# A softmax's inverse sums, spread over the partitions by a round trip through DRAM instead of by transposes

## The chip, the core and the metric

The kernel runs on one core of a Trainium2 chip. The core has TensorE (PE, with its weight loads PEld), VectorE (DVE), ScalarE (ACT), GpSimd (POOL) and SyncE (SP); SP and POOL issue the DMAs of this kernel. The metric is the device time of one execution in microseconds. A measurement runs the kernel several times; a profiled execution gives the trace.

## The reference

One encoder block on 2048 tokens of width 1024 with 16 meta tokens ahead of them (2064 in all), in fp32. The part that matters here is the attention: 4 query heads, 2 key and value heads of 128 channels.

```python
def attend(qb):
    s = jnp.einsum('bkgqd,bksd->bkgqs', qb, kt).astype(jnp.float32) * scale
    p = jax.nn.softmax(s, axis=-1).astype(vt.dtype)
    return jnp.einsum('bkgqs,bksd->bkgqd', p, vt)
...
mixed = jnp.concatenate([rms_norm(attn, g_attn_out[i]), rms_norm(four, g_fourier_out[i])], axis=-1)
h = h + mixed @ w_out[i]
m = rms_norm(h, g_mlp[i])
h = h + jnp.square(jax.nn.relu(m @ w_up[i])) @ w_down[i]
```

A Fourier mixing of the other half of the projection stands beside the attention. A normalization at the end gives the output.

## The kernel before, in words

The kernel first projects, normalizes and rotates q, k and v and parks them in DRAM. Then comes the stage of the attention, from about 345 to 990 us, and after it the MLP, whose products take the rest of the time. In the attention stage the units of the attention are interleaved with other work: the Fourier products (`py`, `pa`), then the output projection of the Fourier half (`out_f`, matmuls `pof`, residual tiles `xo`), then that of the attention half (`out_a`, matmuls `poa`, residual tiles `h`). `mix` steps the attention's generator so many steps for each step of the other work.

There are 16 units. A unit is one key and value head with 512 columns: 256 query tokens of 2 heads. The scores `s` of a unit are made transposed, keys on the partitions and queries on the free axis, in 17 steps of 128 keys (the last one is the meta tokens). ScalarE copies each step to `S`; VectorE keeps the running maximum `M` (L783 to L788). When all are there, `stats` turns the maximum over keys into a tile `mb` that has it in every partition. Then `softmax` walks the 17 steps again: VectorE subtracts `mb` (L840), ScalarE takes the exponential (L841), VectorE adds two steps at a time into `acc` (L845, L847), and TensorE multiplies by the values into the PSUM tile `o` (L849). Scores run a unit and a few steps ahead of this.

At a unit's end, `acc` is folded to `sum` (L827, L828), which still has a partial sum in each of the 128 partitions for each of the 512 columns. `finish(u)` is a generator that runs beside the next unit's steps:

1. ScalarE copies the PSUM tile to `O` (L855).
2. `over_keys` (L794, L796) transposes `sum` in four matmuls against the identity into the PSUM tile `pm_l`, and VectorE reduces it to 128 x 4. VectorE's reciprocal makes `rl` of it (L859): the inverse sum of column 128 a + p stands in partition p, place a.
3. `rows_to_cols` (L803) spreads `rl` again: four more transposes of broadcast columns into the PSUM tile `pd_l`, 128 x 512, which has all 512 inverse sums in every partition.
4. VectorE multiplies `O` by it (L861).
5. The result is split into a high and a low part `ohl` (L870 stores them to the DRAM tile `o_d`), and its squares are summed (L872 to L879).

A `yield` stands between these parts; each lets one more step of the next unit be written into the program. `pm_m`, `pd_m`, `pm_l`, `pd_l` and the sums of squares of `out_f` share one PSUM tile, `misc`. The order on each engine is made by a scheduler from the order in which the code is written; each engine runs its own list in order, and SP its list of DMAs in order too. On SP stand, in this stage, the stores of `o_d`, the loads `at` of the attention's output, the loads `xo` and `h` and the stores `h_d` of the residual, the stores `m_d`, and weight loads. POOL issues the loads of q, k and v.

Of the kernel before, what the change touches and what calls it, by code (L numbers as in the profile page):

```python
# [11 lines left out]
F32 = mybir.dt.float32  # L12
R32 = mybir.dt.float32r
AF = mybir.ActivationFunctionType
ALU = mybir.AluOpType
# [4 lines left out]
P = 128  # L20
# [36 lines left out]
def f32v(ap):  # L57
    return ap.bitcast(F32)
# [30 lines left out]
def bc(ap, shape):  # L89
    return ap.broadcast_to(shape)  # L90
# [45 lines left out]
def encoder_block(ctx: ExitStack, tc: tile.TileContext, x, meta, w_in, w_f,  # L136
                  w_out, w_up, w_down, g_fin, g_cols, g_rows, c_id, c_rope, c_dft, c_even, c_odd, c_rem, out):
    nc = tc.nc
# [7 lines left out]
    dram = ctx.enter_context(tc.tile_pool(name="dram", bufs=1, space=DRAM))  # L146
# [445 lines left out]
    for j in range(LAST + 1):  # L592
# [16 lines left out]
        else:  # L609
# [14 lines left out]
            a = 0  # L624
# [67 lines left out]
    ap2 = Lines(tc.alloc_tile_pool(name="ap2", bufs=1, side="right", reuse_waits="tile"), small)  # L692

    def misc(name, shape=(P, 512)):
        return app.tile(list(shape), F32, name=name, tag="misc")
# [18 lines left out]
        return vt  # L714

    o_d = [dram.tile([P, 2, NQ, 512], F32, name=f"o_d{b}") for b in range(4)]
    sqs = {}
    AT = {}

    def a_operand(b, heads):  # L720

        if b not in AT:
            A = AT[b] = ey.tile([P, 2, NQ, 512], R32, name=f"at_{b}", tag=f"e{b % 2}")
            for k in heads:
                for e in range(2):
                    nc.sync.dma_start(f32v(A[:, e, k]), o_d[b][:, e, k])
        return AT[b]

    def attention():
# [60 lines left out]
        def over_keys(x, name, op):  # L790

            ps = misc("pm_" + name, (P, 4, P))
            for a in range(4):
                nc.tensor.transpose(ps[:, a], x[:, a * P:(a + 1) * P], ident)  # L794
            r = ap2.tile([P, 4], F32, name="mx_" + name, tag="mx", bufs=2)
            nc.vector.tensor_reduce(r, ps, axis=AX.X, op=op)  # L796
            return r

        def rows_to_cols(vec, name):

            ps = misc("pd_" + name, (P, 4, P))
            for a in range(4):
                nc.tensor.transpose(ps[:, a], bc(vec[:, a:a + 1], [P, P]), ident)  # L803
            return ps.rearrange("p a e -> p (a e)")
# [46 lines left out]
        def finish(u):  # L851
            b, g = units[u]
            s = state.pop(u)
            O = ap2.tile([P, 512], F32, name=f"O_{u}", tag="Osb", bufs=1)
            nc.scalar.copy(O, s["O"])  # L855
            yield
            sl = over_keys(s["sum"], f"l{u}", ALU.add)
            rl = ap2.tile([P, 4], F32, name=f"rl_{u}", tag="rl", bufs=2)
            nc.vector.reciprocal(rl, sl)  # L859
            yield  # L860
            nc.vector.tensor_tensor(O, O, rows_to_cols(rl, f"l{u}"), op=ALU.mult)  # L861
            c = slice(b % 2 * 256, b % 2 * 256 + 256)
            if u >= len(units) - 2:
                A = a_operand(3, (2, 3))
                split(A[:, 0, 2 * g:2 * g + 2, c], A[:, 1, 2 * g:2 * g + 2, c], O.rearrange("p (h n) -> p h n", h=2))
            else:
                hl = ap2.tile([P, 2, 512], R32, name=f"ohl_{u}", tag="ohl", bufs=1)
                split(hl[:, 0], hl[:, 1], O)
                for e in range(2):
                    nc.sync.dma_start(o_d[b // 2][:, e, 2 * g:2 * g + 2, c],  # L870
                                      f32v(hl[:, e]).rearrange("p (h n) -> p h n", h=2))
            nc.scalar.square(O, O)  # L872
            first = b not in sqs
            if first:
                sqs[b] = ap2.tile([P, 256], F32, name=f"sq_{b}", tag="sq", bufs=6)
                nc.vector.tensor_tensor(sqs[b], O[:, :256], O[:, 256:], op=ALU.add)
            else:
                for h in range(2):
                    nc.vector.tensor_tensor(sqs[b], sqs[b], O[:, h * 256:(h + 1) * 256], op=ALU.add)  # L879
# [27 lines left out]
        for n in range(total):  # L907
            u, i = divmod(n, K)
            for g in list(later):
                if next(g, "end") == "end":  # L910
                    later.remove(g)
            softmax(u, i)
            loads_next("v", u, i)
            if i == NT:
                later.append(finish(u))
                next(later[-1])
            more(n + 1 + K + LEADT)
            yield
# [816 lines left out]
```

## Time and profile before

| what | us |
|---|---|
| median of 3 runs | 2256.97 |
| the three runs | 2256.97, 3771.39, 2255.45 |
| the profiled execution's own time | 2255.64 |
| its span, first to last instruction | 2253.6 |
| start of the first and of the last transpose of L803 for `pd_l` | 385.0, 988.2 |

The run of 3771.39 stands alone and no profile was taken of it. The profile's lines come from one execution; the span leaves out 2.0 us around the first and the last instruction. In the lines that follow, a group of instructions has its engine, the line of the program, the operation, what it writes and reads, and the durations; a line of the timeline begins with its start and duration in us. A matmul's duration reaches past the start of the next one, since matmuls are pipelined. A line of the windows gives the stretch, its length, and the busy time of each engine with the number of instructions.

### The profile page before, as it was taken

What the parts mean: (1) busy time and instruction counts of PE and PEld (TensorE: products, weight loads), DVE (VectorE), ACT (ScalarE), POOL (GpSimd) and SP (SyncE); (2) the same over time, 40 slices, a digit from 0 to 9 for tenths busy, and PEclk for the clock granted to TensorE, in tenths of its full rate; (3) what the DMA queues carried; (4) which work ended last, traced back from release to release, by engine and by line L of the source; (5) the groups of instructions that cost most, each with busy time, mean ns of one, the idle gap of its engine ahead of it and who ended that gap; (6) DMA issues with size and microseconds to landing.
All of it is one profiled execution on the core that took longest, in us unless ns stands there. A gap on an engine that the chain in (4) does not pass through costs nothing.

```text
span 2253.6 us, 28116 instructions
## 1 busy us (share of the span) xinstructions
PE 2233.3 (99%) x10238; PEld 1771.3 (79%) x10238; DVE 1692.9 (75%) x2250; ACT 1178.1 (52%) x1997; POOL 247.8 (11%) x285
## 2 busy tenths in 40 slices
PE   9999999999999999999999999999999999999998
PEld 7898987766667666677888888888888888888887
DVE  6334579999999889788677668788765656796795
ACT  6443356666555566668556563334455545443343
POOL 2212120003322122110000020000110000200000
PEclk9999999999999999999999999999999999999999
DMA  6332253123344434357777576445594444954342
GB/s 205 90 108 70 86 149 90 52 65 130 113 133 131 158 128 133 137 208 256 264 233 241 181 290 227 132 143 167 185 362 169 154 154 152 343 178 159 126 137 84
DMA packets 191786, 367.40 MB, mean 163 GB/s; under 512 B 15760, under 2 KB 74768, under 8 KB 189984
## 3 DMA queue, kind: packets, MB, share of 16 engines
q1 hardware_dynamic: 171040, 310.08, 40.8%
q0 software_dynamic: 20464, 55.27, 7.6%
q8 instruction: 80, 1.31, 0.2%
q14 instruction: 58, 0.48, 0.1%
q10 hardware_dynamic: 144, 0.26, 0.0%
HBM read 236.28 MB, written 129.27 MB: 162 GB/s over the span
## 4 chain that ended last, share of the span: by engine, by line
PE 89%; DVE 5%; ACT 2%; DMA 1%; issue 1%; POOL 1%; SPq 0%; POOLq 0%; ACTq 0%; DVEq 0%
PE o L849 7%; PE ux L82 5%; PE ux L80 5%; PE ux L81 5%; PE dx L82 5%; PE dx L81 5%; PE dx L80 5%; PE dy L82 4%; PE dy L81 4%; PE dy L80 4%; PE uy L82 4%; PE uy L80 4%; PE uy L81 4%; PE s L80 2%; PE s L82 2%; PE s L81 2%
## 5 line engine op out<-in xcount | busy, mean ns | idle before, releaser
L70 ACT CAST ah<-a 128x1024 fp32r<-128x1024 f32 x108 | 113.0, 1050 | 263.2 <-PE dx L81 108.5
L849 PE MATMUL o<-S,vn 128*128 128x512 f32 x512 | 243.6, 596 | 4.2 <-ACT S L841 3.4
L780 ACT COPY S<-s 128x512 f32<-128x512 f32 x256 | 145.0, 584 | 92.4 <-PE s L82 73.1
L82 PE MATMUL dx<-bh,al 128*128 128x512 f32 x496 | 192.5, 388 | 0.0
L81 PE MATMUL dx<-bl,ah 128*128 128x512 f32 x496 | 192.5, 388 | 0.0
L80 PE MATMUL dx<-bh,ah 128*128 128x512 f32 x496 | 192.5, 388 | 0.0
L82 PE MATMUL ux<-bf,wul 128*128 128x512 f32 x448 | 174.2, 389 | 0.7 <-DVE wul L71 0.7
L80 PE MATMUL ux<-bf,wuh 128*128 128x512 f32 x448 | 174.6, 390 | 0.0
L81 PE MATMUL ux<-bf,wuh 128*128 128x512 f32 x448 | 174.3, 389 | 0.0
L840 DVE TENSOR_TENSOR S<-S,mb 128x1024 f32<-128x1024 f32 x128 | 155.1, 1227 | 11.7 <-ACT mb L811 11.6
L841 ACT ACTIVATE S<-S 128x1024 f32<-128x1024 f32 x128 | 135.1, 1062 | 43.0 <-DVE S L840 41.8
L71 DVE TENSOR_TENSOR al<-a,ah 128x1024 fp32r<-128x1024 f32 x108 | 131.2, 1219 | 31.6 <-ACT ah L70 31.3
L849 PEld LDWEIGHTS o<-S,vn 128*128 128x128 f32 x512 | 92.1, 189 | 75.2 <-issue 59.0
L80 PE MATMUL dy<-bh,ah 128*128 128x512 f32 (+1 forms) x388 | 150.5, 388 | 0.0
L81 PE MATMUL dy<-bl,ah 128*128 128x512 f32 (+1 forms) x388 | 150.5, 388 | 0.0
L82 PE MATMUL dy<-bh,al 128*128 128x512 f32 (+1 forms) x388 | 150.5, 388 | 0.0
L80 PE MATMUL s<-q,kt 128*128 128x512 f32 (+1 forms) x272 | 145.3, 534 | 2.3 <-ACT S L780 2.0
L80 PE MATMUL uy<-bf,wuh 128*128 128x512 f32 x320 | 125.0, 391 | 0.3 <-ACT wuh L70 0.3
L82 PE MATMUL uy<-bf,wul 128*128 128x512 f32 x320 | 124.6, 390 | 0.7 <-DVE wul L71 0.7
L81 PE MATMUL uy<-bf,wuh 128*128 128x512 f32 x320 | 124.8, 390 | 0.0
L786 DVE TENSOR_TENSOR M<-M,S 128x1024 f32<-128x1024 f32 x96 | 117.6, 1225 | 8.9 <-ACT S L780 8.0
L1212 ACT ACTIVATE c<-c 128x512 f32<-128x512 f32 x96 | 60.5, 631 | 119.4 <-DVE c L1260 116.6
(323 smaller groups left out, 5708.3 us busy)
## 6 DMA issues: line engine op xcount, KB each, us to landing
a<-s_d SPq DMA_DIRECT2D x84, 512.0 KB, 3.7
R<-in_w_up_dram SPq DMA_DIRECT2D x32, 1024.0 KB, 5.5
s_d<-s SPq DMA_DIRECT2D x128, 256.0 KB, 2.1
s_d<-c SPq DMA_DIRECT2D x96, 256.0 KB, 2.7
d<-in_w_down_dram SPq DMA_DIRECT2D x48, 512.0 KB, 5.2
f_d<-lf SPq DMA_DIRECT2D x56, 256.0 KB, 2.8
bf<-f_d SPq DMA_DIRECT2D x7, 2048.0 KB, 14.3
a<-s_d POOLq DMA_DIRECT2D x24, 512.0 KB, 7.3
```

What stands on the lines that cost most here:

```text
L70: self.high = nc.scalar.copy(hi, src)
L71: self.low = nc.vector.tensor_tensor(lo, src, f32v(hi), op=ALU.subtract)
L80: nc.tensor.matmul(out, a[0], b[0], start=first, stop=False, skip_group_check=chain)
L81: nc.tensor.matmul(out, a[0], b[1], start=False, stop=False, skip_group_check=chain)
L82: nc.tensor.matmul(out, a[1], b[0], start=False, stop=last, skip_group_check=chain)
L780: nc.scalar.copy(S[:, i % 2], ps)
L786: nc.vector.tensor_tensor(M, M, S, op=ALU.max)
L840: nc.vector.tensor_tensor(S, S, mb, op=ALU.subtract)
L841: nc.scalar.activation(p, S, AF.Exp, scale=ISQ)
L849: nc.tensor.matmul(s["O"], v[:, 2 * j % 4 + e], p[:, e], start=i + e == 1, stop=False)
L1212: nc.scalar.activation(dst, src, AF.Relu)
```

## The change

In the first 15 units, part 3 is replaced. `rl` is written to a row of 512 floats in DRAM, one such row for each unit, element by element: partition p, place a goes to place 128 a + p. A second DMA reads that row back into all 128 partitions of a new SBUF tile `rb`. Both are issued by SP, and the second waits until the first has landed. The generator then yields three times instead of once before the product, so that two more steps of the next unit are written ahead of it. The last unit does as before.

```diff
+    l_d = [dram.tile([1, 512], F32, name=f"l_d{u}") for u in range(15)]
...
             nc.vector.reciprocal(rl, sl)
-            yield
-            nc.vector.tensor_tensor(O, O, rows_to_cols(rl, f"l{u}"), op=ALU.mult)
+            if u < len(l_d):
+                nc.sync.dma_start(l_d[u].rearrange("o (a p) -> p (o a)", p=P), rl)
+                over = ap2.tile([P, 512], F32, name=f"rb_{u}", tag="rb", bufs=1)
+                nc.sync.dma_start(over, l_d[u].broadcast_to([P, 512]))
+                for _ in range(3):
+                    yield
+            else:
+                yield
+                over = rows_to_cols(rl, f"l{u}")
+            nc.vector.tensor_tensor(O, O, over, op=ALU.mult)
```

The scheduler then orders the engines anew in this stage. On TensorE, around the group of unit 1, before (`pd_l1` is the group, `py2` a Fourier product, `o_2` the product with the values of unit 2):

```order
L82 MATMUL s_3_5_4374<-q_3_4133,kt_2_1_3789 128x512
L849 MATMUL o_2_4340<-S_2_0_3929,vn_2_0_4036 128x512
L803 MATMUL pd_l1_4350<-ident_96,rl_1_4337 128x128 x4
L849 MATMUL o_2_4340<-S_2_0_3929,vn_2_0_4036 128x512
L82 MATMUL py2_2_0_4380<-thi2_3_4069,alo2_3_4112 128x258
```

and now:

```order
L795 MATMUL pm_l1_4343<-ident_96,sum_1_4329 128x128 x4
L81 MATMUL py2_2_0_4382<-tlo2_3_4084,ahi2_3_4123 128x258
L82 MATMUL py2_2_0_4382<-thi2_3_4082,alo2_3_4125 128x258
L850 MATMUL o_2_4356<-S_2_0_3944,vn_2_0_4049 128x512 x2
L587 MATMUL py2_2_0_4382<-thi2_4_4088,ahi2_4_4132 128x258
```

The group is gone, and the two matmuls of `o_2` that it parted stand together. On VectorE, from the reciprocal of unit 2 on, before:

```order
L859 RECIPROCAL rl_2_4674<-mx_l2_4672 128x4
L845 TENSOR_TENSOR acc_3_4676<-S_3_0_4260,S_3_2_4328 128x1024
L861 TENSOR_TENSOR O_2_4659<-O_2_4659,pd_l2_4687 128x512
L675 TENSOR_TENSOR EV_70<-C1_0_0_4191,py3_0_0_4709 128x250
L680 TENSOR_TENSOR UA_69<-C1_0_0_4191,py3_0_0_4709 128x258
```

and now:

```order
L860 RECIPROCAL rl_2_4685<-mx_l2_4683 128x4
L680 TENSOR_TENSOR UA_69<-C1_0_1_4220,py3_0_1_4725 128x258
L846 TENSOR_TENSOR acc_3_4690<-S_3_0_4273,S_3_2_4341 128x1024
L787 TENSOR_TENSOR M_4_4699<-M_4_4699,S_4_4_4707 128x1024
L841 TENSOR_TENSOR S_3_4_4372<-S_3_4_4372,mb_3_4646 128x1024
L841 TENSOR_TENSOR S_3_6_4430<-S_3_6_4430,mb_3_4646 128x1024
L870 TENSOR_TENSOR O_2_4670<-O_2_4670,rb_2_4688 128x512
```

Five instructions stand between the reciprocal and the product where one stood. On SP, around the end of unit 3, before (`wfr` and `wor` are weight loads, `o_d0` the store of the unit's output):

```order
L870 DMA o_d0_3413<-ohl_2_4693 128x2x256 x2
L939 DMA xo_0_5086<-in_x_dram 128x1024
L870 DMA o_d0_3413<-ohl_3_5018 128x2x256
L930 DMA wfr0_0_5099<-in_w_out_dram 128x512
L870 DMA o_d0_3413<-ohl_3_5018 128x2x256
L930 DMA wfr0_1_5105<-in_w_out_dram 128x512
```

and now:

```order
L879 DMA o_d0_3413<-ohl_2_4750 128x2x256 x2
L862 DMA l_d3_3420<-rl_3_4974 128x4x1
L948 DMA xo_0_5093<-in_x_dram 128x1024
L939 DMA wfr0_0_5106<-in_w_out_dram 128x512
L864 DMA rb_3_4977<-l_d3_3420 128x512
L939 DMA wfr0_1_5112<-in_w_out_dram 128x512
```

In unit 3 the write and the read of the round trip have two loads between them; in most other units the read stands right behind the write. The stores of `o_d` of this unit come six rows later than the read. After the attention stage the order is that of before.

## The prediction

> **What bounds the kernel.** I read the page first: who is busy and what the chain that ended last is made of.
>
> ```profile
> PE 2233.3 (99%) x10238; PEld 1771.3 (79%) x10238; DVE 1692.9 (75%) x2250; ACT 1178.1 (52%) x1997; POOL 247.8 (11%) x285
> ...
> PE 89%; DVE 5%; ACT 2%; DMA 1%; issue 1%; POOL 1%; SPq 0%; POOLq 0%; ACTq 0%; DVEq 0%
> ```
>
> TensorE sets the end nearly everywhere: 89% of the chain. The change touches only the attention units, so next come the windows of that stage (units 0 to 4, then 5 to 14) and the stage's own chain.
>
> ```profile
> core 0: us, PE busy (x) PEld busy (x) DVE busy (x) ACT busy (x) POOL busy (x), PEclk, DMA share, GB/s
> 381.00:540.00 159.00, 156.28 (x722) 108.33 (x721) 156.00 (x193) 102.73 (x168) 16.12 (x17) 1.00 0.27 82
> 540.00:960.00 420.00, 416.50 (x1650) 284.86 (x1649) 378.71 (x470) 251.11 (x424) 100.66 (x87) 1.00 0.39 130
> ...
> by line: PE o L849 23.5%; PE s L80 7.0%; PE s L82 6.6%; PE s L81 6.6%; DVE S L840 3.7%; PE pof L82 3.5%; PE pof L80 3.5%; PE pof L81 3.5%; issue 3.4%; DVE acc L847 3.2%; DVE M L786 2.3%; POOL rs_m L192 2.1%; PE poa L80 1.8%; PE poa L82 1.7%
> ```
>
> The granted clock is 1.00. In the first stretch VectorE is as full as TensorE (156.00 of 159 us), in the second it has 41 us of 420 to spare. In the chain of 345 to 990 us the TensorE lines shown add to 57.7%, the others shown to 14.7%; 57.7 of 72.4 is 0.80, and I take that for the unnamed rest too. So about four fifths of a TensorE saving is on the path here, less while VectorE is full.
>
> **Removed: fifteen groups of four transposes.** How long one takes, and who waited for it:
>
> ```profile
> L803 PE MATMUL pd_l<-ident,rl x64: 270/273/294, 385.4 to 988.3; 128*128 128x128 f32 x64
> ...
>   DVE O L861: 0.9, 1
> ```
>
> Matmuls overlap, so a group costs what it shifts the next start by. Units 1, 2 and 7, the group and its neighbours:
>
> ```profile
> 420.82 1.02 PE L849 MATMUL o<-S,vn 128*128 128x512 f32 x2
> 421.68 0.60 PE L803 MATMUL pd_l<-ident,rl 128*128 128x128 f32 x4
> 422.12 1.02 PE L849 MATMUL o<-S,vn 128*128 128x512 f32 x2
> ...
> 460.29 0.68 PE L81 MATMUL py<-tlo,ahi 128*128 128x258 f32 x1
> 460.86 0.62 PE L803 MATMUL pd_l<-ident,rl 128*128 128x128 f32 x4
> 461.24 0.37 PE L82 MATMUL py<-thi,alo 128*128 128x258 f32 x1
> ...
> 666.82 0.60 PE L803 MATMUL pd_l<-ident,rl 128*128 128x128 f32 x4
> 667.18 0.47 PE L81 MATMUL s<-q,kt 128*128 128x512 f32 x1
> ```
>
> From the group's first start to the next matmul's start: 0.44, 0.38 and 0.36 us. In unit 2 the group also began late, 0.57 after a matmul that else hands over after 0.12, so it cost 0.83. Read the same way, units 0 to 4 give 2.5 us and units 5 to 14 give 3.9: 6.4 us. The weight loads lie beside it. On the path: 3.9 x 0.8 = 3.1, and for units 0 to 4, where VectorE is just as full, I take half of 2.5, that is 1.25. Together -4.4; bounds 0 (VectorE paces everywhere) and -6.4.
>
> The Trainium skill ("TensorE: Matmul & The Clock Gate", Part 4: PE-mode transpose) has a transpose at about 275 ns in a kernel's context. The trace agrees on that duration, 273 ns, but not as a price: starts are about 0.11 apart.
>
> **Moved: the product that scales O.** It used to read PSUM and now reads SBUF. The nearest row with both operands in SBUF is the sum over two accumulators:
>
> ```profile
> L861 DVE TENSOR_TENSOR O<-O,pd_l x16: 668/678/689, 386.1 to 988.7; 128x512 f32<-128x512 f32 x16
> ...
> L861 DVE TENSOR_TENSOR O<-O,pd_l 128x512 f32<-128x512 f32 x16 | 10.9, 680 | 1.1 <-PE pd_l L803 0.9
> ...
> L827 DVE TENSOR_TENSOR sum<-acc 128x512 f32<-128x512 f32 x16 | 11.3, 705 | 0.2
> ```
>
> 680 against 705 ns: between 0 and 15 x 0.025 = 0.4 us, taken as 0. The casts, squares and sums behind it go along unchanged; their cover is that the stores to o_d are read much later. If that were gone, the loads of the attention output into at would be late.
>
> **Added: a DMA round trip per unit, and VectorE waiting for it.** The write takes 512 pieces of 4 bytes, and no row here has that. The stores of this stage and a store of 1024 pieces (512 KB) bound it; for the read, 256 KB into 128 partitions, there are a quiet load and the loads of at, which queue behind each other:
>
> ```profile
> L870 SPq DMA_DIRECT2D o_d<-ohl x28: 360/371/400, 387.4 to 928.3; - x28
> ...
> DMA to landing us min/median/max: 2.1/2.2/4.7
> ...
> L445 SPq DMA_DIRECT2D q_d<-qt x16: 513/520/1241, 55.5 to 317.5; - x16
> ...
> DMA to landing us min/median/max: 3.5/3.9/8.6
> ...
> traw<-c_odd SPq DMA_DIRECT2D x1, 258.0 KB, 2.6
> ...
> DMA to landing us min/median/max: 3.1/4.7/7.4
> ```
>
> (The last line is that of the at loads.) Write 2.1 to 3.5, taken as 2.3, since 2 KB of payload is nearer the small store; read 2.6 to 4.7, taken as 2.6, since it usually goes out alone; 0.2 for the hand-overs. T = 5.1 us from the reciprocal's end; bounds 4.9 and 8.4.
>
> Against it stands VectorE's own work between the reciprocal and the product, which the two extra yields have made longer. Start-to-start times of such work:
>
> ```profile
> 420.81 0.17 DVE L859 RECIPROCAL rl<-mx_l 128x4 f32<-128x4 f32 x1
> 420.90 1.19 DVE L783 TENSOR_TENSOR M<-S,S 128x1024 f32<-128x1024 f32 x1
> 422.02 1.22 DVE L845 TENSOR_TENSOR acc<-S,S 128x1024 f32<-128x1024 f32 x1
> 423.16 0.68 DVE L861 TENSOR_TENSOR O<-O,pd_l 128x512 f32<-128x512 f32 x1
> 423.76 1.22 DVE L786 TENSOR_TENSOR M<-M,S 128x1024 f32<-128x1024 f32 x1
> ...
> 462.34 0.41 DVE L675 TENSOR_TENSOR EV<-C,py 128x250 f32<-128x250 f32 x1
> 462.66 0.42 DVE L680 TENSOR_TENSOR UA<-C,py 128x258 f32<-128x258 f32 x1
> ...
> 664.06 0.74 DVE L981 SCALAR_TENSOR_TENSOR xo<-pof,rs_f,xo 128x512 f32<-128x512 f32 x1
> 664.72 0.68 DVE L796 TENSOR_REDUCE mx_l<-pm_l 128x4 f32<-128x512 f32 x1
> ```
>
> 1.13 for 128x1024, 0.60 for 128x512, 0.32 for 128x258, 0.66 for the residual update. Before, one or two rows stood between (unit 1: 2.35 us from reciprocal to product). In the changed order unit 1 has five of 1.13 = 5.65, unit 2 has 0.32 + 4 x 1.13 = 4.84, less 0.08 by which they overlap the reciprocal. Counted so, the fifteen covers run from 4.76 (unit 2) to 7.56 (unit 10), mean 5.83. At T = 5.1 only unit 2 waits, 0.3 us.
>
> In unit 3 the read stands behind two loads on SP, of which the weight load stood here before:
>
> ```profile
> 496.76 0.17 DVE L859 RECIPROCAL rl<-mx_l 128x4 f32<-128x4 f32 x1
> ...
> 500.94 0.36 SPq L870 DMA_DIRECT2D o_d<-ohl  x1
> 501.40 0.42 SPq L930 DMA_DIRECT2D wfr<-in_w_out_dram  x1
> ```
>
> Its reciprocal ended at 496.9, so with those 768 KB ahead the data may come at 503.5, against a cover to 502.8: 0.7 more. Stalls: +1; bounds 0 and, at T = 8.4, some 38 (the sum of T less each cover).
>
> **Queued behind the new wait.** SP stands at the read until the write has landed, some 2.3 us, fifteen times. Behind it are the stores of o_d and h_d and the loads of xo, at and h:
>
> ```profile
> SPq L985 <- DVE xo L981: 93.2, 10, 14.3
> ...
> SPq L939 <- DMA h_d<-xo: 31.3, 13, 3.3
> ```
>
> SP spends 93 us of this stage waiting for VectorE's result anyway, up to 14.3 at once, and the loads of xo are made a row ahead, so 2.3 us fit in: 0, bounds 0 and +5. POOL's queue is not touched. The moved product also frees its O tile later, but the next unit writes that tile only a whole unit later.
>
> **Sum.** 2255.64 (the profiled execution, 2.0 over its span, 1.3 below the median of 2256.97) - 4.4 + 0 + 1 + 0 = 2252.2, so 2252.
>
> **Rivals.**
> VectorE paces the stage and the transposes were free: for it, 156.00 of 159 us in the first stretch, and only one wait for pd_l; against it, the chain's TensorE share. Gain near 0, stall 1: 2256.
>
> The transposes were worth their full durations: 60 x 0.273 = 16.4 less, 2239. Against it, the starts 0.44 apart. This is what the Trainium skill's 275 ns (same page and section) would give, as an estimate 16.5.
>
> The round trip outlasts the cover (the slower side): VectorE, in order, stands at the product, and the next subtraction, the exponentials and TensorE's o matmuls behind it come late. For it: the covers leave 0.7 us on average, and loads in traffic take 4.7. With the write at 2.3 and the read at 4.7, T = 7.2 and the waits add to 21 us: 2272. Against it: most reads go out with nothing ahead on SP, and DMA's mean share is 0.27 to 0.39. It begins to outweigh the gain at T near 6, and at T = 9.2 (5.83 + 50/15) it makes the kernel 2% slower. The Trainium skill ("DMA: Bandwidth & Descriptors", Latency and other measured facts) puts HBM's access at 0.2 us on average and 2 us at high load; both legs at the high end would, as an estimate, make T 8.7 and the time about 2294. The quiet rows here, 2.1 and 2.6, look like the low end.
>
> **Chances.** Hidden, with most of the gain: 0.55 (2247 to 2255). Transposes free: 0.18. Round trip too long: 0.22, of which 0.04 beyond 2% (2301). Full durations: 0.04. Something the profile does not show, over 2% faster: 0.01. A change under 2% is about what a measurement of this kernel cannot tell from none. The range 2243 to 2275 holds the first two cases and just over half of the third, about 0.85; it takes in the 6.4 us of the full gain and some reordering below, and the stalls of T = 7.2 above. Faster 0.01, same 0.95, slower 0.04.
>
> **What would show it.** Right: 60 fewer transposes; the last product of the stage, at 988.7 before, some 3 us earlier; write and read landing within 2.1 to 3.5 and 2.6 to 4.7 us; almost no VectorE idle time put down to rb. Wrong: several microseconds per unit of VectorE waiting for the DMA of rb; or a stage of unchanged length with TensorE's idle time grown by 6 us; or SP rows for xo or h landing late enough to appear in the chain.

## The result, and the profile after

| | before | after |
|---|---|---|
| median of 6 runs, us | 2257.27 | 2387.45 (2380.8 to 2390.18) |
| ratio, 95% interval | | 1.057 (1.056 to 1.058) |
| span of the profiled execution, us | 2253.6 | 2385.9 |
| start of the last product that scales `O`, us | 988.7 | 1114.9 |

One of the six runs before (3771.39 us) and one of e4's below (2781.29 us) took far longer than the others of the same kernel, and the ratios leave them out. The kernel is 5.7% slower, where 2252 us, next to no change, was forecast. The last row says where: of the 132.3 us that the span has grown by, 126.2 had been lost when the attention's last unit was scaled. The page of the changed kernel, busy times and chain:

```profile
PE 2267.4 (95%) x10178; PEld 1787.2 (75%) x10178; DVE 1691.5 (71%) x2250; ACT 1178.9 (49%) x1997; POOL 230.9 (10%) x285
...
PE 78%; DMA 10%; DVE 6%; issue 2%; ACT 2%; POOL 1%; SPq 0%; POOLq 0%; DVEq 0%; ACTq 0%
DMA l_d<-rl 6%; PE o L850 5%; PE dx L80 5%; PE dx L81 5%; PE dx L82 5%; PE ux L82 5%; PE ux L80 5%; PE ux L81 5%; PE dy L80 4%; PE dy L81 4%; PE dy L82 4%; PE uy L82 3%; PE uy L80 3%; PE uy L81 3%; DMA rb<-l_d 2%
```

The 60 matmuls are gone as planned. DMA has risen from 1% to 10% of the chain, and the write of 2 KB (`l_d<-rl`) alone is 6% of it. The waits of VectorE, SP and TensorE, one line of each (total us, times, longest); the last line is TensorE's in the kernel before:

```profile
DVE O L870 <- DMA rb<-l_d: 124.4, 15, 11.9
...
SPq L864 <- DMA l_d<-rl: 132.5, 15, 10.3
...
PE s L80 <- ACT S L781: 77.9, 20, 8.6
...
PE s L80 <- ACT S L780: 2.0, 4, 0.8
```

VectorE waits at the product in every unit, 8.3 us on average; TensorE's line of scores waits 77.9 us where it waited 2.0 before. How long the two DMAs take from issue to landing (write, then read):

```profile
L862 SPq DMA_DIRECT2D l_d<-rl x15: 359/371/1175, 384.5 to 1079.7; - x15
...
DMA to landing us min/median/max: 7.8/10.2/11.4
...
L864 SPq DMA_DIRECT2D rb<-l_d x15: 319/320/332, 393.2 to 1089.0; - x15
...
DMA to landing us min/median/max: 3.3/4.7/5.7
```

Two kilobytes need 10.2 us, more than twice the 4.7 of the 256 KB behind them. One unit shows what that does. VectorE's timeline (start, duration, what, and in brackets the idle time before it):

```profile
430.81 0.16 DVE L860 RECIPROCAL rl<-mx_l 128x4 f32<-128x4 f32 x1
430.90 1.18 DVE L787 TENSOR_TENSOR M<-M,S 128x1024 f32<-128x1024 f32 x1
432.01 1.21 DVE L841 TENSOR_TENSOR S<-S,mb 128x1024 f32<-128x1024 f32 x1
433.14 1.21 DVE L846 TENSOR_TENSOR acc<-S,S 128x1024 f32<-128x1024 f32 x1
434.28 1.21 DVE L841 TENSOR_TENSOR S<-S,mb 128x1024 f32<-128x1024 f32 x1
435.42 1.21 DVE L848 TENSOR_TENSOR acc<-acc,S 128x1024 f32<-128x1024 f32 x1
444.72 0.69 DVE L870 TENSOR_TENSOR O<-O,rb 128x512 f32<-128x512 f32 x1 [8.10 <-DMA rb<-l_d]
445.33 1.22 DVE L787 TENSOR_TENSOR M<-M,S 128x1024 f32<-128x1024 f32 x1
```

The five instructions of cover are there, and end at 436.63. The round trip runs from 430.97 to 444.72, 13.75 us, and VectorE stands for the difference, 8.10. TensorE in the same unit, around its own gap:

```profile
438.10 0.40 PE L82 MATMUL s<-q,kt 128*128 128x512 f32 x1
438.33 0.40 PE L80 MATMUL s<-q,kt 128*128 128x512 f32 x1
...
446.60 0.80 PE L80 MATMUL s<-q,kt 128*128 128x512 f32 x1 [5.70 <-ACT S L781]
...
447.62 0.63 PE L82 MATMUL s<-q,kt 128*128 128x512 f32 x1
448.05 0.63 PE L80 MATMUL s<-q,kt 128*128 128x512 f32 x1
```

Before the gap the scores' matmuls start 0.23 us apart, after it 0.43. The windows of the same kernel explain that (stretch, its length, busy time of PE, PEld, DVE, ACT and POOL, then the granted clock, the DMA share and GB/s); the first line is the stage from 381 us to its end, the others are stretches around this gap:

```profile
381.00:1115.00 734.00, 631.77 (x2409) 424.44 (x2408) 557.59 (x695) 372.37 (x617) 102.87 (x106) 0.93 0.36 101
...
438.00:446.00 8.00, 2.90 (x10) 1.38 (x8) 1.28 (x2) 0.56 (x2) 0.00 (x0) 0.98 0.17 33
446.60:453.40 6.80, 6.80 (x29) 6.22 (x30) 6.80 (x8) 4.22 (x8) 0.00 (x0) 0.57 0.23 77
454.00:462.00 8.00, 8.00 (x26) 4.52 (x25) 7.45 (x11) 5.06 (x9) 0.00 (x0) 1.00 0.13 35
```

After the idle stretch TensorE has 0.57 of its clock on the mean of 6.8 us; shorter windows within it show 0.50 up to 452.0 us and 1.00 from 453.4 on, so it is half the clock and then the full one. Over the stage the clock that was not granted is 734 x 0.07 = 51 us of full clock; before, the granted clock of this stage was 1.00.

The Trainium skill ("TensorE: Matmul & The Clock Gate", Part 1, HAM oscillation) says that a gap of more than about 3.4 us puts TensorE back to half its clock. The trace agrees: after 5.70 us idle, 0.50.

### The profile page after: what moved, and what is told of

It reads as the page before. It is cut to its first block, busy times and chain, and to the rows that moved or that the text cites. A ratio compares the mean times of both kernels' runs of the same rounds, so it can differ in the third digit from the quotient of the medians.

```text
span 2385.9 us, 28046 instructions
## 1 busy us (share of the span) xinstructions
PE 2267.4 (95%) x10178; PEld 1787.2 (75%) x10178; DVE 1691.5 (71%) x2250; ACT 1178.9 (49%) x1997; POOL 230.9 (10%) x285
## 4 chain that ended last, share of the span: by engine, by line
PE 78%; DMA 10%; DVE 6%; issue 2%; ACT 2%; POOL 1%; SPq 0%; POOLq 0%; DVEq 0%; ACTq 0%
DMA l_d<-rl 6%; PE o L850 5%; PE dx L80 5%; PE dx L81 5%; PE dx L82 5%; PE ux L82 5%; PE ux L80 5%; PE ux L81 5%; PE dy L80 4%; PE dy L81 4%; PE dy L82 4%; PE uy L82 3%; PE uy L80 3%; PE uy L81 3%; DMA rb<-l_d 2%
## 5 line engine op out<-in xcount | busy, mean ns | idle before, releaser
L850 PE MATMUL o<-S,vn 128*128 128x512 f32 x512 | 251.3, 614 | 13.3 <-ACT S L842 12.6
L80 PE MATMUL s<-q,kt 128*128 128x512 f32 (+1 forms) x272 | 147.3, 542 | 78.0 <-ACT S L781 77.9
L80 PEld LDWEIGHTS s<-q,kt 128*128 128x128 f32 (+1 forms) x272 | 53.4, 196 | 120.0 <-ACT S L781 98.8
L848 DVE TENSOR_TENSOR acc<-acc,S 128x1024 f32<-128x1024 f32 x96 | 117.4, 1223 | 7.1 <-ACT S L842 7.0
```

Of the source, the lines that this page charges most:

```text
L80: nc.tensor.matmul(out, a[0], b[0], start=first, stop=False, skip_group_check=chain)
L848: nc.vector.tensor_tensor(acc, acc, p, op=ALU.add)
L850: nc.tensor.matmul(s["O"], v[:, 2 * j % 4 + e], p[:, e], start=i + e == 1, stop=False)
```

## The experiments

The theory: the write is slow because its 512 four-byte pieces lie side by side in 2 KB of DRAM, coming from 128 partitions; VectorE, which runs its list in order, waits for it, and TensorE starves. The rivals: a write of 512 pieces, or a round trip through DRAM, is slow in any layout; the later place of the product costs the time; the missing transposes or SP's standing still cost it. The diffs are shortened and stand against the changed kernel; e15's stands against e11, and e8's shows lines that e8 adds to the kernel before. Each ratio is to the kernel before, run on the same chip.

**e1: the same 2 KB in 128 pieces of 16 bytes.**

```diff
-                nc.sync.dma_start(l_d[u].rearrange("o (a p) -> p (o a)", p=P), rl)
+                nc.sync.dma_start(l_d[u].rearrange("o (p a) -> p (o a)", a=4), rl)
```

> The four sums of a partition go to DRAM as one piece of 16 bytes instead of four of 4 bytes, so 128 pieces instead of 512 into the same 2 KB; the order in the row is another, so the output has other sums in it. If the write's 10.2 us are set by the number of small pieces (about (10.2 - 2.2) / 512 = 16 ns each), or by pieces that meet in the same short stretch of DRAM, it lands in about 4 us, the round trip is 7 to 9 us, VectorE waits 2 to 4 us a unit for rb, and the time is 2275 to 2320. If any DRAM write of pieces this small has a fixed price, it lands in about 10 us and the time stays at 2380 to 2390.

Measured: 2263.63 us, ratio 1.0027 (1.0016 to 1.0038). The instructions of the write's line in e1, and how long they took to land:

```profile
L862 SPq DMA_DIRECT2D l_d<-rl x15: 319/320/953, 384.7 to 966.1; - x15
...
DMA to landing us min/median/max: 1.4/1.7/3.3
```

1.7 us in place of 10.2, and VectorE waits 8.8 us for `rb` in all; both the 4 and the 10 us of that text were too much. A round trip through DRAM is not slow as such, nor is a write to these rows. But pieces became both fewer and larger, so e1 does not say which counts.

**e2 and e11: 512 pieces of 4 bytes again, but 512 bytes apart.** Both write into a scratch buffer. In e2 the four values of a partition are neighbours there. e11, whose diff follows, keeps the order and shape of the changed kernel's write (`a p`: neighbours come from neighbouring partitions), and only the spacing differs. Both read back 2 KB of the scratch buffer that lie together, so their output is not scaled by the sums.

```diff
-    l_d = [dram.tile([1, 512], F32, name=f"l_d{u}") for u in range(15)]
+    l_d = range(15)
+    l_far = dram.tile([4, P, P], F32, name="l_far")
...
-                nc.sync.dma_start(l_d[u].rearrange("o (a p) -> p (o a)", p=P), rl)
+                nc.sync.dma_start(l_far[:, :, 0:1].rearrange("a p o -> p (a o)"), rl)
...
-                nc.sync.dma_start(over, l_d[u].broadcast_to([P, 512]))
+                nc.sync.dma_start(over, l_far[0:1, 0:4].rearrange("o a e -> o (a e)").broadcast_to([P, 512]))
```

> As many 4-byte pieces as in the changed kernel (512), but each 512 bytes from the next in DRAM, so that no two meet; the read takes 2 KB of that area, which does not hold the inverse sums but one of them and zeros. If pieces that meet in the same stretch of DRAM hold each other up, the write lands in 2 to 3 us, VectorE waits 1 to 3 us a unit, and the time is 2260 to 2300. If the number of small pieces sets it, or their size alone, it lands in about 10 us as before and the time stays at 2380 to 2390.

> The 512 pieces of 4 bytes are written in the same order, by the same engines and with the same shape as in the changed kernel (column 128 a + p from partition p), but 512 bytes from one another. The output is not scaled by the sums, since the read takes 2 KB of that area. If lying side by side in DRAM is the cause, the write lands in 2 to 3 us and the time is 2255 to 2270. If it is the order in which the partitions' pieces go out, or the shape of the transfer, it lands in about 10 us and the time is above 2370.

Measured: e2 2260.01 us, 1.0015 (1.0006 to 1.0024), its write lands after 2.1/2.3/3.8 us. e11 2258.22 us, 1.0003 (0.9994 to 1.0012). In e11, the instructions of the write's line and of the read's, with those who waited for the read (us, times):

```profile
L866 SPq DMA_DIRECT2D l_far<-rl x15: 359/371/762, 384.9 to 965.0; - x15
...
DMA to landing us min/median/max: 1.8/1.9/3.5
...
L868 SPq DMA_DIRECT2D rb<-l_far x15: 319/320/385, 386.8 to 967.4; - x15
...
  DVE O L874: 6.7, 6
...
DMA to landing us min/median/max: 3.0/3.2/6.2
```

As many pieces, as small, in the same order: 1.9 us instead of 10.2, and the whole loss is gone. Neither the count nor the size nor the order of the pieces makes the write slow by itself; 512 pieces of 4 bytes are slow where they lie side by side. Lying side by side is not enough either: the 128 pieces of e1 do, and are fast. The product stands as late as in the changed kernel, so its place is no cause either.

**e10: 8 bytes apart, partition by partition.** In this order the four pieces of a partition are neighbours. The read again takes 2 KB of the scratch buffer.

```diff
+    l_far = dram.tile([P, 4, 2], F32, name="l_far")
...
-                nc.sync.dma_start(l_d[u].rearrange("o (a p) -> p (o a)", p=P), rl)
+                nc.sync.dma_start(l_far[:, :, 0:1].rearrange("p a o -> p (a o)"), rl)
```

> 512 pieces of 4 bytes, 8 bytes from one another and in the order of the partitions, so that the pieces one DMA engine writes lie side by side and a line of 64 bytes is written by one engine alone; in the changed kernel pieces of neighbouring partitions share a line and the four pieces of a partition lie 512 bytes apart. The output is not scaled by the sums but by what stands in 2 KB of that area. If pieces meeting in a line of 64 bytes hold each other up whoever writes them, the write lands in 6 to 10 us and the time is above 2310. If only pieces from different engines do, it lands in 2 to 3 us and the time is 2255 to 2275.

Measured: 2287.86 us, 1.0138 (1.0125 to 1.0152). The instructions of the write's line in e10 and their landing:

```profile
L866 SPq DMA_DIRECT2D l_far<-rl x15: 524/525/1105, 385.0 to 990.9; - x15
...
DMA to landing us min/median/max: 3.2/4.5/6.3
```

Neither of the two outcomes of that text: 4.5 us, and VectorE waits 35.3 us for `rb`. Its stretch of 64 bytes is an assumption that no run here measures. Counted by pieces in each 512 bytes (128, 64, 32 and 1 in the changed kernel, e10, e1 and e11), the medians are 10.2, 4.5, 1.7 and 1.9 us. So it looks like crowding; but order, count or size change along the way, and the runs do not tell how the time falls with the distance alone.

The Trainium skill ("DMA: Bandwidth & Descriptors", Specifications) has transfers below 512 bytes written by reading and writing back. Taken alone that would make the pieces of e11 as slow as those of the changed kernel; the runs show 1.9 against 10.2. That neighbouring pieces wait for one another there would fit both, but the pieces of e1, 16 bytes side by side, land in 1.7, and no run shows the mechanism.

**e4 and e5: the change's other parts.** e4 has no spreading in the 15 units at all (the product reads another tile of the same size, `mb`); its diff follows. e5 keeps the transposes and takes from the change only its three yields.

```diff
-                nc.sync.dma_start(l_d[u].rearrange("o (a p) -> p (o a)", p=P), rl)
-                over = ap2.tile([P, 512], F32, name=f"rb_{u}", tag="rb", bufs=1)
-                nc.sync.dma_start(over, l_d[u].broadcast_to([P, 512]))
-                for _ in range(3):
-                    yield
+                over = s["mb"]
+                yield
```

> The four transposes of a unit are left out in the first 15 units and nothing takes their place: O is multiplied by the tile mb, which lies in SBUF anyway, so the output is not scaled by the sums. By the prediction's own term the time is 4.4 us under that of before (bounds 0 and 6.4): 2249 to 2256. If the transposes were worth their full durations, 16 us: about 2240. If VectorE paces the stage, no difference at all.

> The four transposes stay and no DMA is added; only the three yields of the change are kept, so the product stands as far behind the reciprocal as in the changed kernel. If the new order of the engines is harmless by itself, the time is within 6 us of that before (2251 to 2263) and none of the 130 us belongs to it. If the later product costs something through ohl, the squares or the one-buffer tiles, it is above 2265.

Measured: e4 2253.37 us, 0.9986 (0.9977 to 0.9995); e5 2254.21 us, 0.9987 (0.9979 to 0.9996). Without spreading the kernel gains 3.2 us (1.1 to 5.2). The later product costs nothing: e5, with the transposes in place, is 2.9 us below before by its ratio (0.9 to 4.7), and the fastest kernel here that computes everything. Since a new order alone moves the time by as much, the 3.2 us of e4 are not cleanly the transposes' own.

**e12: the slow write alone.** e4 with the write of the changed kernel put back; nobody reads it, and no engine waits for its data.

```diff
-                over = ap2.tile([P, 512], F32, name=f"rb_{u}", tag="rb", bufs=1)
-                nc.sync.dma_start(over, l_d[u].broadcast_to([P, 512]))
-                for _ in range(3):
-                    yield
+                over = s["mb"]
+                yield
```

> Only the slow write is added to the run without transposes and without a round trip (2253): nobody reads the row, no instruction waits for it, and O is multiplied by mb, so the output is not scaled by the sums. If the slow write also holds up the transfers that SP issues behind it, as the landings of 12 to 17 us behind it suggest, the time is 2265 to 2285, and those loads appear in the chain of waits. If a slow write costs only the instruction that waits for it, the time is 2250 to 2257.

Measured: 2278.34 us, 1.0092 (1.0078 to 1.0105), 25.0 us over e4 (24 by their ratios to before). Some long pieces of its chain (start, us, what):

```profile
882.77 4.36 DMA h_d<-h
...
936.90 10.28 DMA o_d<-ohl
947.67 4.16 DMA h_d<-h
...
1014.18 5.51 DMA h_d<-h
```

The 15 unread writes of 2 KB still cost 1%. ScalarE's waits for the residual's stores in e12, and before:

```profile
ACT h L1076 <- DMA h_d<-h: 22.6, 5, 9.5
...
ACT h L1069 <- DMA h_d<-h: 2.9, 3, 1.3
```

The store of `o_d` at 936.90, which takes 2.2 us in the kernel before, was issued 2.3 us behind a slow write and took 10.28. The windows of the changed kernel show what such transfers do meanwhile: at 525.6 and 526.1 the loads of `xo` and a weight were issued behind the write of 525.1, which landed at 536.5 (columns as above):

```profile
526.00:536.00 10.00, 5.63 (x15) 2.41 (x14) 5.07 (x5) 4.07 (x9) 2.96 (x3) 0.92 1.01 32
537.00:545.00 8.00, 4.78 (x9) 3.02 (x10) 3.44 (x4) 5.35 (x9) 0.00 (x0) 0.52 1.05 347
```

The 16 DMA engines count as fully busy in both (shares of 1.01 and 1.05), but move 32 GB/s while the write is outstanding and 347 after it. In the traces of the changed kernel, e3, e9 and e12, 89 DMAs of SP or of POOL were issued between the issue of a slow write and its landing, as far as the traces show both landings: none landed before the write did. For 75 of the 89 the write still had longer to go than the same transfer takes in the kernel before (the median there), so this is not only a matter of a late start.

The Trainium skill ("DMA: Bandwidth & Descriptors", Queues, rings and completion order) says that the signal of a DMA's end lands only after every earlier write of the same DMA engine, across its queues. The 0 of 89 agree. The 32 GB/s say more, that the data themselves were held up; the same page (Back-pressure in remote DMA) has stalled writes stall an engine's other queues, told there of transfers between cores, and these windows look like it within one core.

**e3 and e9: keep the slow round trip, take VectorE's wait away.** e3 yields 12 times instead of 3 and issues the product behind the running unit's last accumulation, so that 13 to 25 instructions lie between reciprocal and product. e9 also lets POOL issue the read, so that SP does not stand.

```diff
-                for _ in range(3):
+                for _ in range(12):
...
-            nc.vector.tensor_tensor(O, O, over, op=ALU.mult)
+            with tc.issue_after(state["acc"]) if u < len(l_d) else nullcontext():
+                nc.vector.tensor_tensor(O, O, over, op=ALU.mult)
```

> The round trip is unchanged, but the product that needs it stands 13 to 25 VectorE instructions behind the reciprocal instead of 5 to 11. If VectorE's wait, and the idle TensorE and lower clock that follow from it, are the whole loss, the write still lands in about 10 us, the wait for rb falls from 124 us to under 10, the clock is 1.0 again and the time is 2247 to 2260. If SP standing still for 10 us in each unit, or the DRAM writes themselves, cost anything of weight, it stays above 2275.

> As in the run with the late product (2286), the write is the slow one on SP and the product stands far behind, but the read is issued by POOL, so that POOL waits for the write and SP does not. If SP standing for 10 us in each unit, with the loads and stores behind it, is what kept that run 29 us above the time of before, the time falls to 2255 to 2268. If the slow write itself, its traffic or the late product are to blame, it stays within 6 us of 2286. If POOL standing delays the loads of q, k and v in the same way, it is above 2268, and waits for kt or vn show it.

Measured: e3 2286.02 us, 1.0127 (1.0114 to 1.014); e9 2283.04 us, 1.0118 (1.0103 to 1.0134). The waits in e3, VectorE's, SP's and two of ScalarE's:

```profile
DVE O L871 <- DMA rb<-l_d: 7.7, 2, 4.6
...
SPq L864 <- DMA l_d<-rl: 131.2, 15, 10.4
...
ACT h L1079 <- DMA h_d<-h: 27.0, 6, 7.8
ACT wfh L73 <- DMA wfr<-in_w_out_dram: 9.0, 1, 9.0
```

VectorE's wait falls from 124.4 to 7.7 us and the time by 101 us, to some 8 us above the unread write of e12; the mean granted clock is back at 0.995, from 0.977. So VectorE's wait, with the idle TensorE and the lower clock behind it, was about four fifths of the loss. The rest shows as transfers that come late: ScalarE waits 27.0 us for the store of `h_d`, 2.9 before. SP's standing still 131 us is not what costs: in e9 SP does not stand, and the time is within 3 us of e3's. There POOL stands instead:

```profile
POOL rb L864 <- DMA l_d<-rl: 182.2, 13, 23.9
```

So e9 alone would leave standing still in doubt; but in e12 no issuer waits for the write, and 25 of the 33 us that e3 lies above e4 are there.

**e7: one transpose back, so that the write has 4 pieces of 512 bytes.** A version with a complete output. TensorE transposes `rl` to 4 x 128, ScalarE copies it to SBUF, and the write takes rows.

```diff
-                nc.sync.dma_start(l_d[u].rearrange("o (a p) -> p (o a)", p=P), rl)
+                rt = misc(f"rt_{u}", (4, P))
+                nc.tensor.transpose(rt, rl, ident)
+                rr = ap2.tile([4, P], F32, name=f"rr_{u}", tag="rr", bufs=1)
+                nc.scalar.copy(rr, rt)
+                nc.sync.dma_start(l_d[u].rearrange("o (a p) -> (o a) p", p=P), rr)
```

> Still the round trip, with the right result: one transpose turns the 128 x 4 inverse sums into 4 rows of 128, ScalarE copies them to SBUF, and the write is 4 pieces of 512 bytes instead of 512 of 4. If scattered words side by side are what made the write slow, it lands in 2 to 2.5 us; the transpose and the copy add 1 to 2 us ahead of it; VectorE waits 1 to 3 us a unit and the time is 2262 to 2285. If a write to DRAM from 4 partitions is slow in itself, it lands later than 4 us and the time is above 2290.

Measured: 2261.97 us, 1.0024 (1.0014 to 1.0033). VectorE waits 2.2 us for `rb` in all, in 3 units. The trace does not give this write's landing; the read, which waits for it, is issued 1.2 to 2.6 us after the write. This mends the loss, but the round trip is still no better than the four transposes.

**e8: summing and spreading in one matmul with a matrix of ones.** It sums over the partitions and spreads the sum at once; VectorE then takes the reciprocal of 128 x 512 instead of 128 x 4.

```diff
+            total = misc(f"lt_{u}")
+            nc.tensor.matmul(total, every, s["sum"], start=True, stop=True)
+            yield
+            over = ap2.tile([P, 512], F32, name=f"rb_{u}", tag="rb", bufs=1)
+            nc.vector.reciprocal(over, total)
```

> Neither transposes nor a round trip for the sums, in all 16 units: one matmul of the partial sums against a 128 x 128 tile of ones puts each column's sum into every partition at once; VectorE takes the reciprocal of 128 x 512 and multiplies. TensorE gives up eight transposes (0.88 us by their spacing) for one matmul of 0.43, VectorE a reduction and a small reciprocal (0.8 us) for a large reciprocal (0.6 to 0.7, if it runs as its other work of this size does). By the terms that held so far (about 3 us for 6.4 us of TensorE time) the time is 2248 to 2256, at or a little under the kernel before. If a large reciprocal is much slower than other work of its size, it is above 2260.

Measured: 2273.18 us, 1.0068 (1.0055 to 1.0082). The row of the reciprocal, with its durations (least, median, most, in ns):

```profile
L863 DVE RECIPROCAL rb<-lt x16: 3334/3351/3358, 382.7 to 1005.1; 128x512 f32<-128x512 f32 x16
```

3351 ns, 6.5 ns a column; 16 of them are 54 us on an engine that is full in the first units. The seven matmuls that each unit saves by it don't make up for that: 16 us slower.

**e15: e11 with the product held back.** Six yields, and the product behind the running unit's last accumulation.

```diff
-                for _ in range(3):
+                for _ in range(6):
...
-            nc.vector.tensor_tensor(O, O, over, op=ALU.mult)
+            with tc.issue_after(state["acc"]) if u < 15 else nullcontext():
+                nc.vector.tensor_tensor(O, O, over, op=ALU.mult)
```

> The round trip with its pieces 512 B apart, as in e11_apart_order, and the multiplication by the spread inverse sums held back until the running unit's last accumulation is issued, so that some instructions more stand between the reciprocal and the product. In e11 the product waited 6.7 us in all for the DMA of rb (6 times), and e11 is 4.9 us above the kernel without any spreading (2258.2 against 2253.4). If those waits are what the round trip still costs, they fall to about 1 us and the time comes out at 2251 to 2255 us (2258.2 less 3 to 7). If what is left is the SP queue standing for 2 us per unit, or the later product itself, the time stays at 2257 to 2261 us although the waits for rb are gone. The output is complete; the write is of pieces 512 B apart in a larger scratch buffer.

That text calls the output complete; it is not: as in e11, the read takes 2 KB of the scratch buffer, in which only 4 of the 512 values lie. Measured: 2259.19 us, 1.0004 (0.9995 to 1.0013). VectorE's waits, the line of the product:

```profile
DVE O L875 <- DMA rb<-l_far: 1.9, 2, 1.0
```

The waits are gone and the time has not fallen: the ratio is 1.0004 after 1.0003. What is left of the round trip, some 5 us against e4, is not VectorE's wait. Whether it is the 256 KB per unit beside other transfers, or SP standing, stays open.

| kernel | us | ratio | write lands, us | VectorE waits for `rb`, us | last product, us |
|---|---|---|---|---|---|
| before | 2257.27 | | | | 988.7 |
| changed | 2387.45 | 1.057 | 10.2 | 124.4 | 1114.9 |
| e3: slow write, product late | 2286.02 | 1.0127 | 10.1 | 7.7 | 1014.8 |
| e12: slow write, unread | 2278.34 | 1.0092 | 10.6 | none | 1008.6 |
| e1: 128 pieces of 16 B | 2263.63 | 1.0027 | 1.7 | 8.8 | 991.5 |
| e11: 512 B apart | 2258.22 | 1.0003 | 1.9 | 6.7 | 990.3 |
| e4: no spreading | 2253.37 | 0.9986 | | none | 982.3 |

In steps: -3.2 (1.1 to 5.2) for the transposes, from before to e4; +25 for the slow write and what queues behind it, from e4 to e12; +109 for VectorE's wait and its consequences, the read's own cost among them, from e12 to the changed kernel. The mean granted clock is 0.994 in e12 and 0.977 in the changed kernel, which makes 14 and 55 us not granted over the spans of 2279.5 and 2385.9; so the lower clock can be at most 41 of the 109, and how much of these lay on the path was not separated.

## Why the prediction was wrong, point by point

**The step that failed** is the size of one term: "Write 2.1 to 3.5, taken as 2.3, since 2 KB of payload is nearer the small store". It took 7.8 to 11.4 us, median 10.2. The prediction said itself that no row here has 512 pieces of 4 bytes, and then bounded it by rows whose pieces are long. Payload was the wrong measure of nearness, and the upper bound of 3.5 was no bound: it is the least landing of its own row, 3.5/3.9/8.6. e11 shows that the term would have been right, at 1.9, for pieces that lie apart.

**"read 2.6 to 4.7, taken as 2.6"**: measured 3.3 to 5.7, median 4.7. The high end was the better guess, and it too was no bound, but the median of its row, 3.1/4.7/7.4; the same read in e11 took 3.2. With the longest of both rows, 8.6 and 7.4, T would have been 16.2, far past the 9.2 at which the prediction saw 2%.

**VectorE's cover** came out as counted: 5.65 us in unit 1, and there it ended 5.66 us after the reciprocal did. With the true durations the prediction's own formula gives about the measured wait: from the reciprocal's end to the product the 15 units take 13.5 to 18.1 us, mean 14.5; less the mean cover of 5.83, times 15, that is 130; measured 124.4.

**The term for what queues behind the new wait, "0, bounds 0 and +5"**, failed too. It counted how long SP stands, 2.3 us a time, and not what the DMA engines do for transfers already issued. SP stood 132.5 us, and e9 and e12 show that this is not what costs; but the slow write held up the transfers behind it, +25 us in e12, with nobody waiting for its data.

**The transposes, -4.4**: -3.2 in e4, inside the bounds of 0 and -6.4. The last product there starts 6.4 us earlier, the full shift that was counted, of which half is lost again by the end. As e5 moves the time by nearly as much through the order alone, the term is borne out in size only. **The moved product, 0**: 0.69 us against 0.68, and e5 shows that its later place does not cost.

**The rival that came true** is the round trip that outlasts the cover. Its mechanism was right, and a mean T of 14.5 with a loss of 5.7% fits its point of decision (2% slower from T = 9.2); its time of 2272 was not, since it put only the read at its high end. It had a chance of 0.22, and past 2% only 0.04. It counted one us of VectorE's wait as one us of time, and that held: e10 has 28.6 us more of these waits than e11 and takes some 30 us longer, and the 124.4 us of the changed kernel came to 109. The half clock behind TensorE's gaps, which the prediction does not have, lies within these 109.

**What would show it wrong** was named as "several microseconds per unit of VectorE waiting for the DMA of rb"; 8.3 us a unit is that line of the profile.

## What to carry to other kernels

Bound a DMA by rows with pieces of the same length and spacing, not of the same payload, and by the longest of a row, not its least; where the trace has none, keep the range wide. Do not write single words side by side from many partitions to DRAM: transpose first so that each piece is a row, as in e7. Distance between the words makes the write fast too, but e11 reads no words that lie apart, and what such a read takes was not measured. A slow DMA cost twice here, through whoever waits for it and through every transfer issued behind it; and a wait in the middle of an engine that runs in order needs a cover that is longer than the slowest landing.

## What the runs showed of the hardware

- 512 words of 4 bytes land in 10.2 us when they fill 2 KB of DRAM side by side, in 1.9 us when they lie 512 bytes apart in the same order, and in 1.7 us as 128 pieces of 16 bytes side by side.
- Behind such a write other transfers of the core crawl (32 GB/s against 347) and none of 89 landed before it, whichever of SP and POOL had issued them.
- After a gap of 5.70 us TensorE's granted clock was 0.50 for some 6 us more, then 1.00.
- VectorE's reciprocal takes 6.5 ns a column (3351 ns for 128 x 512), a product of the same size 0.68 us.
